# Two transformer blocks on one core: convolution transposes a step later, one step a group in the output norm, Fourier columns first

## The chip, the cores and the metric

The kernel runs on one core of one Trainium2 chip. The metric is the device time in microseconds of one execution; lower is better. Three executions of the kernel before took 2638.27 to 2641.5 us, with a median of 2640.46 us.

## The reference

Two blocks work on a sequence of 256 rows of 2048 float32 values.

The first block is two layers. A layer projects its input to 7680 columns and makes three branches: differential attention (4 heads), dilated attention (8 heads) and a gated convolution of 31 taps with a norm and a pointwise projection. Each branch is gated, the three are joined, projected back, added to the input and normed.

```python
def conformer_conv(u, glu_gate, w_dw, b_dw, ln_g, ln_b, w_pw):
    h = u * jax.nn.sigmoid(glu_gate)
    h = lax.conv_general_dilated(h, w_dw[:, None, :], ...) + b_dw
    h = jax.nn.silu(layer_norm(h, ln_g, ln_b))
    return h @ w_pw
...
    y = jnp.concatenate([ya, yb, yc], axis=-1) @ w_out
    return layer_norm(ALPHA * x + y, ln_g, ln_b)
```

The second block first makes six vectors (shifts, scales, gates) from a condition vector and a large matrix `w_mod`. It norms its input and a context, projects both, and mixes four branches: neighbourhood attention with the context (8 heads), a Fourier transform, pooling windows and a short convolution. Then come a gated merge, a projection and a feed-forward part.

```python
    h = modulate(rms_norm(x, norm1_w[i]), sh1, sc1)
    q, k, v, ft, pool, sv, sb, sc = mixer_inputs(h, w_in[i], q_norm_w[i], k_norm_w[i])
    branches = (neighbourhood_attention(q, k, v, kc, vc, rpb[i]), fourier_mix(ft),
                pool_mix(pool, w_pool[i], pool_scale[i]), short_conv_mix(sv, sb, sc, conv_w[i]))
```

## The kernel before

All large products are "blocks": 256 rows times 512 output columns. A float32 product is made of three fast products: weights and activations are each split in a rounded part `hi` and a rest `lo`, and hi x hi, hi x lo and lo x hi are accumulated in one PSUM bank. So TensorE works through a list of "jobs" (256 rows of a weight block, 12 matmuls of 512 columns), and `run` (L326) issues one step for each: 12 matmuls and what belongs around them.

In a step `run` issues, in this order: `high` (ScalarE rounds the weights of the job four steps ahead, L343), one step of each running task (`step_tasks`, L211), `low` (VectorE makes the rest, L351) and the load of a later weight tile on SP's queue, one product pair of the modulation where the meter leaves room (`wmod_step`, L438), and the step's 12 matmuls, with the block's `pre` ahead of its first and its evacuation behind its last (L374 to L400). Every engine runs its own instructions in the order in which they were issued.

The small work (heads, convolution, norms, transposes) is written as tasks: Python generators whose `yield` ends what they issue in one step. `step_tasks` takes tasks from the front of a queue while the running ones hold under 3 of the PSUM banks kept for them (and enough of the 13 scratch rows), and steps each. `need` (L184) forces a task: all that it has left is issued at once, in the step in which something needs it. All of these groups therefore stand at places in the engines' queues that follow from counts of yields.

The meter: VectorE's and TensorE's estimated times are added up when instructions are issued (L61 to L76), each step lays 1.15 on VectorE's (SPLIT, L359), and `room` (L177) is what is left of a lead of 2.6.

```python
    def room(self):
        return self.t_pe + 2.6 - self.t_dve
```

The modulation: `WMOD_STEPS` (L37) spreads the 32 jobs of each of six chunks over steps. A job of a chunk that begins at a and ends at b is due at a + (b - a) x number/32; it is issued when its step is at or past the due one and the room is at least 1.0 (chunks 0 and 1, two VectorE products a job) or 0.2 (the others, one product), and eight steps past due in any case (L450). Chunk 0 is (22, 146), chunk 1 (160, 274).

Where the change touches:

- `conv` (L925) is the convolution of a layer as a task. The evacuation of the layer's second block adds it (`ev_glu`, L590, which also makes the gated product `sg` on VectorE). It transposes `sg` (L935), copies it to `pad`, then makes 124 tap products, two or four in a step: `if i % 4 == 3 or i % 2 and self.room() < 0.9: yield`, each laid to the meter as 0.33. Then it transposes, norms, transposes back, and makes the pair `cT` (`cTh` at L985 on ScalarE, a yield, `cTl` at L987 on VectorE). The block `conv_pw` (L647) needs that pair: its `pre` forces the task. It is the 13th block of the layer; the 12 ahead of it are 8 steps each. A layer has 154 steps.
- `layer_end` (L690) for layer 1: the task `gen` (L747) norms the layer's output in place (`norm`, L694), multiplies and adds the rows `ln_g` and `ln_b` (`affine`, four VectorE products a group; the rows come by GpSimd's queue, `row`, L711), sums squares (`square`), stores each group (`keep`, L723, also on GpSimd's queue), and then goes on in `rms_t` (L780): sums, scale by ScalarE (`xr`), transposes, and the pairs `hT`. Its steps run beside the four blocks on the context (`kc0`, `vc0`, `kc1`, `vc1`, 32 steps), which are the first of the second block.
- `second` (L991): behind the context blocks come the blocks on `hT`: keys, values, queries of four heads (`k0`, `v0`, `q0`), the Fourier columns (`w[6]`), and keys, values, queries of the other four. The first of them forces `hT` as far as it needs it (`h_pre`). The evacuation of a query block adds four tasks `na_head` (L1045, 23 steps each, after a wait for the normed queries) and a task that forces these heads and then transposes their output. The evacuation of the Fourier block puts two tasks `fourier_groups` (13 steps each) at the front of the queue (L1336).

Of the kernel before, what the change touches and what calls it, by code (L numbers as in the profile page):

```python
# [128 lines left out]
class Kernel:  # L129
# [560 lines left out]
    def layer_end(self, l, r, stats):  # L690
        nc, a = self.nc, self.a
        mv, rs = stats["mv"], stats["rs"]

        def norm(g, t):  # L694
            if len(rs) <= t:
                return None
            if g == 0:
                nc.vector.tensor_scalar(r[g][:, t], r[g][:, t], mv[:, t, 0:1], rs[t][0][:, 0:1],
                                        op0=ALU.subtract, op1=ALU.mult)
            else:  # L700
                nc.scalar.activation(r[g][:, t], r[g][:, t], AF.Identity, scale=rs[t][0][:, 0:1], bias=rs[t][1])
            return r[g][:, t]

        if l == 0 and len(rs) == 1:
            self.xs = self.dp.tile([S, D], F32, name="xs0")
        elif l == 1:
            self.xs = self.dp.tile([S, D], F32, name="xs1")
        xs = self.xs
        rows = {}

        def row(g):  # L711
            if g < 4 and g not in rows:
                rows[g] = []
                for nm_ in ("ln_g", "ln_b"):
                    q = self.h([128, 512], name="row")
                    nc.gpsimd.dma_start(q, a[nm_][l:l + 1, g * 512:(g + 1) * 512].broadcast_to([128, 512]))
                    rows[g].append(q)

        def affine(g, t):
            nc.vector.tensor_tensor(r[g][:, t], r[g][:, t], rows[g][0], op=ALU.mult)  # L720
            nc.vector.tensor_tensor(r[g][:, t], r[g][:, t], rows[g][1], op=ALU.add)

        def keep(g):  # L723
            nc.gpsimd.dma_start(xs[:, g * 512:(g + 1) * 512].rearrange("(t p) f -> p t f", p=128), r[g])

        if l == 0 and len(rs) == 2:
            def gen():
                yield from self.wait(lambda: self.x_task, [self.xT_task])
                for g in range(4):
                    row(g)  # L730
                    yield
                    for t in range(2):
                        while self.room() < 0.6 and not self.x_task.forced:
                            yield
                        affine(g, t)
                        yield
                    keep(g)
            self.x_task = self.add(gen(), banks=0, rows=4)
        elif l == 0:
            self.xT = [self.pair("xT") for _ in range(4)]  # L740
            self.xT_task = self.add(self.split_t(
                [self.t_items(g, self.xT[g], norm, self.col("lng", g * 4, 4), self.col("lnb", g * 4, 4))[t]
                 for g, t in TILES], ahead=2), front=True)
        else:
            ss = self.m([128, 2, 4], name="ss")

            def gen():  # L747
                row(0)
                row(1)
                for g in range(6):  # L750
                    if g < 4:
                        for t in range(2):
                            norm(g, t)
                    if g >= 2:
                        for t in range(2):
                            self.square(r[g - 2][:, t], ss[:, t, g - 2:g - 1])
                        keep(g - 2)
                    yield
                    if 1 <= g < 5:
                        for t in range(2):  # L760
                            affine(g - 1, t)
                        yield
                        rows.pop(g - 1)
                        row(g + 1)
                yield from self.rms_t(r, ss, "sc1", "sh1")
            self.hT = [self.pair("hT") for _ in range(4)]
            self.h_dst = self.hT
            self.hT_task = self.add(gen(), front=True, rows=7)
        self.x_in = xs
# [155 lines left out]
    def conv(self, l, h, st):  # L925
        nc = self.nc
        hp = self.cp.tile([128, 4, 30 + S], F32, name="pad")
        nc.gpsimd.memset(hp[:, :, 0:30], 0.0)
        yield
        for c in range(0, 4, 2):  # L930
            p = self.aux()
            for i in range(2):
                for t in range(2):
                    o = i * 256 + t * 128
                    nc.tensor.transpose(p[:, o:o + 128], h[:, t, (c + i) * 128:(c + i + 1) * 128], self.ident)  # L935
            yield
            nc.scalar.activation(hp[:, c:c + 2, 30:30 + S], p.rearrange("p (c t) -> p c t", c=2), AF.Copy)
            yield
        acc = self.s([128, 4, S], name="cacc")
        st["conv"].banks = 0  # L940
        for i in range(4 * TAPS):
            j, c = divmod(i, 4)
            wj = self.col(f"dw{l}", c * TAPS + j)
            x = hp[:, c, j:j + S]
            if j == 0:
                nc.vector.tensor_scalar(acc[:, c], x, wj, self.col(f"cb{l}", c), op0=ALU.mult, op1=ALU.add)
            else:
                nc.vector.scalar_tensor_tensor(acc[:, c], x, wj, acc[:, c], op0=ALU.mult, op1=ALU.add)
            if i % 4 == 3 or i % 2 and self.room() < 0.9:
                yield  # L950
        yield
        while self.held()[1] >= 3 and not st["conv"].forced:
            yield
        st["conv"].banks = 1
        z = self.s([128, 2, 512], name="z")
        for t in range(2):
            p = self.aux()
            for c in range(4):
                nc.tensor.transpose(p[:, c * 128:(c + 1) * 128], acc[:, c, t * 128:(t + 1) * 128], self.ident)
            yield  # L960
            bn = self.m([128, 6], name="cbn")
            nc.vector.bn_stats(bn, p)
            mv = self.m([128, 2], name="cmv")
            nc.vector.bn_aggr(mv, bn)
            rs = self.rstd(mv[:, 1:2], 1, 1.0, EPS)
            yield
            nm = self.m([128, 1], name="nm")
            nc.vector.scalar_tensor_tensor(nm, mv[:, 0:1], -1.0, rs[:, 0:1], op0=ALU.mult, op1=ALU.mult)
            nc.scalar.activation(z[:, t], p, AF.Identity, scale=rs[:, 0:1], bias=nm)
            yield  # L970
        yield
        cT = self.pair("cT")
        u = self.s([128, 4, S], name="csilu")
        for c in range(0, 4, 2):
            p = self.aux()
            for i in range(2):
                for t in range(2):
                    o = i * 256 + t * 128
                    nc.tensor.transpose(p[:, o:o + 128], z[:, t, (c + i) * 128:(c + i + 1) * 128], self.ident)
            yield  # L980
            for i in range(2):
                nc.scalar.activation(u[:, c + i], p[:, i * 256:(i + 1) * 256], AF.Silu,
                                     scale=self.col(f"cg{l}", c + i), bias=self.col(f"cl{l}", c + i))
            yield
        nc.scalar.activation(cT[0], u, AF.Copy)  # L985
        yield
        nc.vector.tensor_tensor(cT[1], u, cT[0], op=ALU.subtract)  # L987
        st["cT"] = cT


    def second(self):  # L991
        nc, a = self.nc, self.a
        w = a["w_in2"]
# [17 lines left out]
        hsrc = lambda k, t: self.src_of(hT)(k, t)  # L1011
# [64 lines left out]
        def ev_branch(key, fn):  # L1076
            def ev(ps):
                ev_copy(key)(ps)
                bT[key] = self.pair("bT")
                st["t" + key] = fn(st.pop(key), bT[key])  # L1080
            return ev
# [2 lines left out]
                                      (2560, ev_copy("vc1")))):  # L1084
            self.block(w[c0 // 512], csrc, ev, start=start_na if i == 0 else None)
        for g in range(2):
            self.block(w[2 + g], hsrc, ev_norm(f"k{g}"), pre=None if g else h_pre,
                       start=None if g else h_start)
            self.block(w[4 + g], hsrc, ev_copy(f"v{g}"))
            self.block(w[g], hsrc, ev_norm(f"q{g}", heads(g)))  # L1090
            if g == 0:
                self.block(w[6], hsrc, ev_branch("ft", self.fourier))

        def ev_sv(ps):
            x = st["sc"]
# [88 lines left out]
        for n in range(4):  # L1184
            self.block(a["w_o"][n], lambda k, t: self.src_of(yT)(k, t), evac_t=ev_o(n),
                       pre=lambda k: self.need(st[f"m{k // 2}"]), start=load_x(n, r, (3, 4, 5) if n == 3 else ()), tail=TAIL if n == 3 else 0)
# [36 lines left out]
        for part, js in ((0, range(0, 4)), (1, range(4, 8)), (2, range(8, 11))):  # L1223
# [3 lines left out]
            for n in range(4):  # L1227
                self.block(a["w_fd"][n], lambda k, t: self.src_of(aT)(k, t), evac_t=ev_down(part, n),
                           pairs=[2 * j + i for j in js for i in range(2)],
                           pre=lambda k: self.need(st[f"f{k // 2}"]), start=load_x(n, xr),  # L1230
# [302 lines left out]
```

## Time and profile before

| | |
|---|---|
| median of 3 executions | 2640.46 us (2638.27 to 2641.5) |
| profiled execution | 2642.78 us |
| its span | 2640.9 us, mean granted TensorE clock 0.996 |
| TensorE busy | 99% of the span |
| VectorE, ScalarE, GpSimd busy | 68%, 48%, 5% |
| mean DMA | 233 GB/s |

The span goes from the first to the last instruction of the profiled execution; the execution's own time lies around it. PE is TensorE's matmuls, PEld its weight loads, DVE is VectorE, ACT is ScalarE, POOL is GpSimd; a q behind an engine's name is its queue of DMAs. [...] Instructions issued through the meter's helper all carry its line, L75, so they are known by their tiles (out<-in). A number in brackets is the time for which the engine sat idle ahead of the instruction, with what released it. Adjacent equal instructions are merged in a timeline (x4).

### The profile page before, as it was taken

The page shows a single profiled execution, that of the slowest core. Times are in us where ns is not written, and L with a number is a line of the kernel's source. Part 1 is how long each engine was busy: PE and PEld are TensorE (multiplying, and loading weights), DVE is VectorE, ACT ScalarE, POOL GpSimd, SP SyncE. Part 2 cuts the span into 40 slices and gives each one's busy share as a digit, 9 for nine tenths or more (in the row PEclk, how much of TensorE's full clock was granted, in tenths as well). Part 3 has the DMA queues.
Part 4 walks back from the last instruction along what each step waited for, and adds up shares of the span by engine and source line. Part 5 has one row for each costly group of instructions (what it writes and reads, how often), then busy time and mean ns, then how long its engine had stood idle before and what let it go on. Part 6 is the DMA issues. An engine that isn't in the chain of part 4 may idle for free.

```text
span 2640.9 us, 32555 instructions
## 1 busy us (share of the span) xinstructions
PE 2611.5 (99%) x11902; PEld 2155.8 (82%) x11902; DVE 1802.6 (68%) x2516; ACT 1257.7 (48%) x1603; POOL 132.0 (5%) x193
## 2 busy tenths in 40 slices
PE   9999999999999999999999999999999999999999
PEld 7888888778888878887888888888788888888887
DVE  5898777799977788655766677777655554555444
ACT  6444753545466555444454444444544434443442
POOL 0000010000001020100200000000100000001000
PEclk9999999899999999999999999999999999999999
DMA  8776676676666788775776787888655576657664
GB/s 303 244 225 213 212 238 232 194 256 223 216 217 218 266 280 280 249 244 177 240 233 242 236 294 258 291 289 312 222 187 194 187 243 201 193 189 240 226 195 152
DMA packets 171233, 614.69 MB, mean 233 GB/s; under 512 B 19849, under 2 KB 20673, under 8 KB 171073
## 3 DMA queue, kind: packets, MB, share of 16 engines
q1 hardware_dynamic: 158400, 572.59, 64.9%
q0 software_dynamic: 11232, 37.24, 4.4%
q10 hardware_dynamic: 1440, 2.79, 0.3%
q8 instruction: 93, 1.52, 0.2%
q14 instruction: 68, 0.55, 0.1%
HBM read 599.92 MB, written 12.62 MB: 232 GB/s over the span
## 4 chain that ended last, share of the span: by engine, by line
PE 94%; DVE 2%; DMA 2%; issue 1%; POOL 0%; ACT 0%; SPq 0%; DVEq 0%; ACTq 0%; POOLq 0%
PE mm L75 88%; PE aux L75 6%; DMA raw<-in_w_in 1%; DVE lo L351 1%; DMA raw<-in_w_out 1%; DMA row<-in_ln_b 1%; DVE f L75 0%; DVE res L75 0%; ACT hi L343 0%; POOL rstd L229 0%; DVE wmjunk L75 0%; POOL rstd L228 0%; DVE xTl L75 0%; DVE gate L75 0%; DVE h2Tl L75 0%
## 5 line engine op out<-in xcount | busy, mean ns | idle before, releaser
L351 DVE TENSOR_TENSOR lo<-raw,hi 128x1024 fp32r<-128x1024 f32 (+1 forms) x893 | 1077.9, 1220 | 641.8 <-ACT hi L343 640.9
L343 ACT ACTIVATE hi<-raw 128x1024 fp32r<-128x1024 f32 (+1 forms) x893 | 936.6, 1059 | 1028.0 <-PE mm L75 832.1
L75 PE MATMUL mm<-hi,xTh 128*128 128x512 f32 x960 | 385.3, 401 | 6.0 <-ACT hi L343 5.9
L75 PE MATMUL mm<-hi,xTl 128*128 128x512 f32 x960 | 377.2, 393 | 1.1 <-DVE xTl L75 1.1
L75 PE MATMUL mm<-lo,xTh 128*128 128x512 f32 x960 | 376.2, 392 | 0.0
L75 PE MATMUL mm<-hi,hTh 128*128 128x512 f32 x864 | 343.6, 398 | 0.0
L75 PE MATMUL mm<-hi,hTl 128*128 128x512 f32 x864 | 336.9, 390 | 0.0
L75 PE MATMUL mm<-lo,hTh 128*128 128x512 f32 x864 | 336.4, 389 | 0.0
L75 DVE CUSTOM_DVE_ANT_0 wmjunk<-wm,c 128x1024 bf16<-128x1024 f32 x256 | 312.4, 1220 | 4.7 <-DMA wm<-in_w_mod 2.4
L75 PE MATMUL mm<-hi,h2Th 128*128 128x512 f32 x704 | 276.0, 392 | 0.1
L75 PE MATMUL mm<-hi,h2Tl 128*128 128x512 f32 x704 | 274.5, 390 | 1.1 <-DVE h2Tl L75 1.1
L75 PE MATMUL mm<-lo,h2Th 128*128 128x512 f32 x704 | 274.3, 390 | 0.0
L75 PEld LDWEIGHTS mm<-hi,xTh 128*128 128x128 f32 x960 | 181.9, 189 | 43.4 <-ACT hi L343 5.9
L75 PEld LDWEIGHTS mm<-hi,xTl 128*128 128x128 f32 x960 | 181.4, 189 | 41.3 <-DVE xTl L75 2.2
L75 PEld LDWEIGHTS mm<-lo,xTh 128*128 128x128 f32 x960 | 181.9, 189 | 35.9 <-DVE lo L351 0.4
L75 PEld LDWEIGHTS mm<-hi,hTl 128*128 128x128 f32 x864 | 162.2, 188 | 34.4
L75 PEld LDWEIGHTS mm<-lo,hTh 128*128 128x128 f32 x864 | 162.4, 188 | 32.8 <-issue 0.2
L75 PEld LDWEIGHTS mm<-hi,hTh 128*128 128x128 f32 x864 | 162.3, 188 | 32.4 <-issue 0.5
L75 PEld LDWEIGHTS mm<-hi,h2Tl 128*128 128x128 f32 x704 | 132.3, 188 | 29.1 <-DVE h2Tl L75 1.5
L75 PEld LDWEIGHTS mm<-hi,h2Th 128*128 128x128 f32 x704 | 132.4, 188 | 27.5 <-ACT h2Th L284 0.8
L75 PEld LDWEIGHTS mm<-lo,h2Th 128*128 128x128 f32 x704 | 132.4, 188 | 26.9
L75 PE MATMUL mm<-hi,yTh 128*128 128x512 f32 x384 | 150.9, 393 | 0.0
(274 smaller groups left out, 3061.0 us busy)
## 6 DMA issues: line engine op xcount, KB each, us to landing
raw<-in_w_in SPq DMA_DIRECT2D x360, 512.0 KB, 4.4
wm<-in_w_mod SPq DMA_DIRECT2D x192, 512.0 KB, 4.8
raw<-in_w_gate SPq DMA_DIRECT2D x128, 512.0 KB, 4.7
raw<-in_w_fg SPq DMA_DIRECT2D x88, 512.0 KB, 4.4
raw<-in_w_fu SPq DMA_DIRECT2D x88, 512.0 KB, 3.8
raw<-in_w_fd SPq DMA_DIRECT2D x88, 512.0 KB, 4.3
raw<-in_w_out SPq DMA_DIRECT2D x64, 512.0 KB, 4.6
raw<-in_w_o SPq DMA_DIRECT2D x32, 512.0 KB, 5.2
```

What stands on the lines that cost most here:

```text
L75: return f(*args, **kw)
L343: nc.scalar.activation(hi[:, k], t[:, k], AF.Copy)
L351: nc.nc.vector.tensor_tensor(lo[:, k], t[:, k], hi[:, k], op=ALU.subtract)
```

## The change

In `conv` one more `yield` stands ahead of the first transposes. In `layer_end`'s task for layer 1, two of a group's yields become one at the group's end, so that the norm of one group, the squares of another and the products of a third are issued in one step. In `second` the Fourier block moves from behind the first queries to the front of the blocks on `hT`, and takes `pre` and `start` with it.

```diff
@@ -755,13 +755,12 @@
                         for t in range(2):
                             self.square(r[g - 2][:, t], ss[:, t, g - 2:g - 1])
                         keep(g - 2)
-                    yield
                     if 1 <= g < 5:
                         for t in range(2):
                             affine(g - 1, t)
-                        yield
                         rows.pop(g - 1)
                         row(g + 1)
+                    yield
                 yield from self.rms_t(r, ss, "sc1", "sh1")
             self.hT = [self.pair("hT") for _ in range(4)]
             self.h_dst = self.hT
@@ -926,6 +925,7 @@
         nc = self.nc
         hp = self.cp.tile([128, 4, 30 + S], F32, name="pad")
         nc.gpsimd.memset(hp[:, :, 0:30], 0.0)
+        yield
         yield
         for c in range(0, 4, 2):
             p = self.aux()
@@ -1084,12 +1084,11 @@
                                       (2560, ev_copy("vc1")))):
             self.block(w[c0 // 512], csrc, ev, start=start_na if i == 0 else None)
         for g in range(2):
-            self.block(w[2 + g], hsrc, ev_norm(f"k{g}"), pre=None if g else h_pre,
-                       start=None if g else h_start)
+            if g == 0:
+                self.block(w[6], hsrc, ev_branch("ft", self.fourier), pre=h_pre, start=h_start)
+            self.block(w[2 + g], hsrc, ev_norm(f"k{g}"))
             self.block(w[4 + g], hsrc, ev_copy(f"v{g}"))
             self.block(w[g], hsrc, ev_norm(f"q{g}", heads(g)))
-            if g == 0:
-                self.block(w[6], hsrc, ev_branch("ft", self.fourier))
```

## Rows read from the trace of the kernel before

**Rows 1.** page, part 1: busy us, share of the span, instructions
```profile
PE 2611.5 (99%) x11902; PEld 2155.8 (82%) x11902; DVE 1802.6 (68%) x2516; ACT 1257.7 (48%) x1603; POOL 132.0 (5%) x193
```

**Rows 2.** waits of TensorE, whole span: us in total, times, longest us
```profile
PE aux L75 <- ACT xr L792: 7.4, 2, 4.4
...
PE aux L75 <- DVE sg L75: 1.8, 2, 1.6
```

**Rows 3.** chain that ended last, one step: start us, us, what
```profile
910.16 2.76 PE mm L75 x12
```

**Rows 4.** timeline, layer 1's gated product: start us, us, instruction, [idle before <-releaser]
```profile
531.16 0.33 PE L75 MATMUL aux<-ident,sg 128*128 128x128 f32 x1 [1.58 <-DVE sg L75]
...
531.75 0.55 PE L75 MATMUL aux<-ident,sg 128*128 128x128 f32 x3 [0.27 <-DVE sg L75]
```

**Rows 5.** timeline, layer 1, where the convolution ends
```profile
765.59 1.05 ACT L985 ACTIVATE cTh<-csilu 128x1024 fp32r<-128x1024 f32 x1
...
767.12 1.22 DVE L75 TENSOR_TENSOR cTl<-csilu,cTh 128x1024 fp32r<-128x1024 f32 x1
...
770.43 1.28 ACT L623 ACTIVATE gate<-mm 128x512 f32<-128x512 f32 x2 [0.19 <-PE mm L75]
...
771.61 1.05 ACT L343 ACTIVATE hi<-raw 128x1024 fp32r<-128x1024 f32 x1
...
772.42 0.40 PE L75 MATMUL mm<-hi,cTl 128*128 128x512 f32 x1
...
772.69 1.23 DVE L351 TENSOR_TENSOR lo<-raw,hi 128x1024 fp32r<-128x1024 f32 x1 [4.35 <-ACT hi L343]
```

**Rows 6.** timeline of VectorE, layer 1's modulation pairs, 1st and 25th
```profile
509.00 1.22 DVE L75 CUSTOM_DVE_ANT_0 wmjunk<-wm,c 128x1024 bf16<-128x1024 f32 x1
...
759.90 1.22 DVE L75 CUSTOM_DVE_ANT_0 wmjunk<-wm,c 128x1024 bf16<-128x1024 f32 x1
```

**Rows 7.** timeline, layer 0: modulation pairs 1 and 19, and the projection
```profile
71.49 1.22 DVE L75 CUSTOM_DVE_ANT_0 wmjunk<-wm,c 128x1024 bf16<-128x1024 f32 x1
...
285.08 1.22 DVE L75 CUSTOM_DVE_ANT_0 wmjunk<-wm,c 128x1024 bf16<-128x1024 f32 x1
...
296.79 1.05 ACT L343 ACTIVATE hi<-raw 128x1024 fp32r<-128x1024 f32 x1
...
297.61 0.40 PE L75 MATMUL mm<-hi,cTl 128*128 128x512 f32 x1
```

**Rows 8.** windows: start:end length, busy PE, PEld, DVE, ACT, POOL, clock, DMA, GB/s
```profile
983.00:986.40 3.40, 0.42 (x3) 0.15 (x2) 2.04 (x2) 0.93 (x2) 3.10 (x4) 1.00 0.58 186
...
1899.00:1906.00 7.00, 5.25 (x20) 3.97 (x20) 6.44 (x16) 5.71 (x10) 1.92 (x4) 0.51 0.74 249
```

**Rows 9.** timeline of TensorE, two waits of transposes for scaled rows
```profile
986.25 0.66 PE L75 MATMUL aux<-ident,xr 128*128 128x128 f32 x4 [2.98 <-ACT xr L792]
...
1900.51 2.82 PE L75 MATMUL aux<-ident,xr 128*128 128x128 f32 x12 [4.40 <-ACT xr L792]
```

**Rows 10.** timeline, first context block and the output norm
```profile
947.75 0.39 PE L75 MATMUL mm<-hi,hcTh 128*128 128x512 f32 x1
...
957.34 2.02 DVE L75 TENSOR_TENSOR res<-res,row 128x512 f32<-128x512 f32 x3 [1.09 <-DMA row<-in_ln_b]
...
962.69 2.74 DVE L75 TENSOR_TENSOR res<-res,row 128x512 f32<-128x512 f32 x4
...
979.76 0.21 DVE L75 TENSOR_REDUCE tot<-ss 128x1 f32<-128x4 f32 x2
```

**Rows 11.** timeline, the second block's first heads
```profile
1203.14 0.48 DVE L75 TENSOR_SCALAR qk<-aux,qns 128x256 f32<-128x256 f32 x1 [3.40 <-PE aux L75]
...
1203.66 0.47 ACT L1276 ACTIVATE qk<-aux,cols 128x256 f32<-128x256 f32 x1 [0.36 <-DVE qk L75]
...
1244.79 0.66 PE L75 MATMUL aux<-ident,sc 128*128 128x128 f32 x4 [1.64 <-ACT sc L1295]
...
1246.14 0.71 PE L75 MATMUL aux<-v,pt 128*128 128x128 f32 x4 [0.69 <-ACT pt L1303]
```

## Prediction

> **What bounds the kernel now.** I read the page first: TensorE is busy 2611.5 of 2640.9 us, so 29.4 us idle [rows 1]. Then the list of what TensorE waited for: besides the start and the layer ends, the places that the edits touch are the scaled rows of the norm (7.4 us in two waits, of which one is touched) and the gated convolution input (1.8 us) [rows 2]. So the time is matrix work plus waits in TensorE's own queue. No edit adds or drops an instruction on any engine; each only places groups of them elsewhere in queues that run in program order. What must be asked of each is which group now stands behind something late. I count the scheduler's steps in the code (one step is 12 large matmuls, 2.76 us [rows 3]) and fix them to the trace where a group shows; step 0 is the first of a layer, or of the second block's own projections.
>
> **Edit 1, convolution one step later.** What it gives: in layer 1 the transposes stand at step 17 and wait 1.58 and 0.27 us for the gated product [rows 4]; those are both of the waits of this kind [rows 2], so layer 0 gives nothing. A step later the product is there. Gain 1.85 us; the bound the other way is 0.
>
> What it costs lies at the other end. The taps take two a step: the meter leaves a room of at most 2.6 - 1.15 - 2 x 0.33 = 0.79, under 0.9, so 124 taps are 62 steps, 21 to 82, and nothing in the loop can catch up. From there the steps are fixed: cTh is issued in step 95 and cTl in step 96. The block that reads the pair, the pointwise projection, begins in step 96 (12 blocks of 8 lie before it). The trace agrees: cTl is the last thing before step 96's weight split, at 767.12, while the first matmul that reads it starts at 772.42; it has 4.1 us to spare [rows 5]. One step later, cTh is issued in step 96 and cTl is forced by the block itself, behind all that step 96 has queued. On ScalarE that is the gate's evacuation, which cannot start before TensorE ends step 95 (770.43, 1.28 us), then the weight split of 771.61 (1.05 us) [rows 5]: cTh runs at about 772.7 to 773.7. On VectorE it is the split of 772.69 and then a pair of modulation products: the pair at 759.90 is the 25th since 509.00 [rows 6], so the next, number 25 counted from 0, falls due at 160 + 114 x 25/32 = 249.06, and step 96 of layer 1 is slot 250. Before, cTl itself took the room that step 96 had; now it is not yet counted and 1.45 is free, over the 1.0 asked. So VectorE goes 773.8 + 2 x 1.22 = 776.3, and cTl ends at 777.5: 5.1 us after TensorE wants it. All of this is on TensorE's path: the three products accumulate in one bank in that order, and everything behind them on its queue waits. Layer 0 is the same: pair 285.08 is the 19th since 71.49, the next is due at 22 + 124 x 19/32 = 95.6, and the split of 296.79 and the matmul at 297.61 [rows 7] lie as in layer 1. Bounds: without the pair in front 2.6 us each; above, half a step more, 6.5, as the convolution's last activations move into step 95, ahead of the gate on ScalarE.
>
> **The clock.** Idle of this length has a second price. [...] The new wait is 5.1 us with two matmuls in it, nearest to the 4.40, so I add half of 5.25, 2.6 us, each; the bound below is 0. [...]
>
> So edit 1: -1.85 + 2 x (5.1 + 2.6) = +13.6 us.
>
> **Edit 2, the norm in one step a group.** Six steps instead of ten before the row sums. It removes the 2.98 us wait of the transposes at 986.25, which came from sums taken at 979.76 and then queued on GpSimd behind another task [rows 9, 10]: the sums now come before that task. But VectorE gets four affine products (2.74 us) and a weight split (1.23) in each of four steps in a row, 3.9 us against TensorE's 2.76. The start does not move: the bias row lands at 957.34 as before (GpSimd issues it at the same place), and three products follow to 959.4 [rows 10]. The splits of steps 1 to 4 of the first context block then end at about 960.5, 964.4, 968.2 and 972.1. TensorE uses them four steps on, from 947.75 + 2.76 k [rows 10]: at 961.8, 964.5, 967.3 and 970.1 for k = 5 to 8 (second matmul of each). So it waits 0.9 and, after that, 1.1 us: 2.0. The weight loads start late with the splits, and the first scaled rows stand on ScalarE behind a split of such a load: 0.5 to 1.8 us more at step 9, taken as 1.2. GpSimd's own queue (row loads, stores of the output) keeps its order; each store waits for the same products as before. Sum 3.2 - 2.98 = +0.2; bounds -2.98 (all of it covered by the four steps in hand) and +5 (the last row, loaded behind the first store, lands late and the clock falls too).
>
> **Edit 3, Fourier first.** The two Fourier tasks ran between the second block's heads 0 to 2 and the pass that transposes their output. They move to steps 10 to 19 of the block, with three steps between the issue of their table loads and the first use; cost 0, or one wait of a step at most if a table came late. But they were what held two of the three task slots while head 3 ran. In the kernel before, the pass starts at step 63, when head 3 has done half, and forces the other half: TensorE waits 1.64 and 0.69 us [rows 11]. Now heads 0 and 1 end at step 57, and at step 58 head 3 and the pass start together, so the pass forces the whole head: the same two waits for its first half, 2.33, and before them the copies of its q and k, 0.48 on VectorE and then 0.47 on ScalarE with hand-overs [rows 11], 1.1. Its bias loads are on GpSimd's queue, which has nothing else there and issues them when their buffers come free, not when TensorE gets to the step: 0. +3.4 us; bounds 0 and +6. The second group has the same order of tasks behind the pool block in both kernels: 0. SP's queue keeps one weight load a step; only whose it is changes.
>
> **Sum.** 13.6 + 0.2 + 3.4 = +17.2 us. The profiled execution took 2642.78 us (span 2640.9), 2.3 over the median 2640.46 of the three runs; it goes to 2660.0, the median to 2657.6. A difference under 0.2% (5.3 us) can't be told from none.
>
> **Rivals.**
> - Clock stays up through both new waits: 2652.4. For it the 2.98 us row and the two matmuls inside the wait; against it the 4.40 us row. Chance 0.19.
> - The modulation pair is not in front of cTl (it depends on the meter's room to a tenth): 2.6 for 5.1 twice, 2652.6. Chance 0.10.
> - The norm is dearer: VectorE is the bound for longer, about 5 us: 2662.4. For it the load that lands at 957.34 with VectorE waiting; against it that modulation products are held back meanwhile. Chance 0.12.
> - Not slower: the pair is in time. Its place is step 96, its price 15.4 us, and it decides at cTl's end before 772.42. It needs ScalarE to run cTh ahead of the gate's evacuation, or a tap step that takes four taps. Then -1.85 + 0.2 + 3.4 = +1.8, 2642.2: no change. Only the 4.1 us to spare speaks for it, more than one step. Chance 0.12.
> - Beyond that, all the waits named go and none comes: -1.85 - 2.98 - 2.33 = -7.2, 2633.3. That the Fourier tasks leave would have to let head 3 end first, and their slots are filled at once. Chance 0.06.
>
> **How the numbers follow.** The forecast has 0.41. Faster is the last rival, 0.06; within 0.2% the one before, 0.12; the rest, 0.82, is slower. The range runs from 2644, where clock and pair are both cheap, to 2666, the dear norm with its bound on the head; it leaves out the last two rivals, 0.18.
>
> **What would show it.** Right: waits of the pointwise matmuls on cTh and then cTl in both layers, about 5 us each, clock rows under 1 behind them; no wait on the gated product; none of 2.98 us before the norm's transposes but small ones on weight splits before; two pairs of 1.64 and 0.69 where one was at the first heads. Wrong: pointwise matmuls that start with no wait, which takes 15 us of the 17 away.

## The result and the profile after the change

The changed kernel takes 2674.52 us (median of three executions, 2674.44 to 2674.63) where the kernel before takes 2640.85 on the same chip, so 33.7 us more by the medians. The ratio is 1.0124 with a 95% interval of 1.011 to 1.0138, which is 32.7 us, 29.0 to 36.4. A fourth execution ran at a granted clock of 0.749 of full speed, took 3307.47 us and is left out. Forecast were 17.2 us more, with a range up to 2666. The direction was right, the size about half, and the time lies outside the range.

The changed kernel's page, part 1 (busy us, share of the span, instructions), to be set beside [rows 1]:

```profile
PE 2621.8 (98%) x11902; PEld 2161.1 (81%) x11902; DVE 1802.9 (67%) x2516; ACT 1258.8 (47%) x1605; POOL 129.7 (5%) x193
```

TensorE issues the same 11902 instructions and is busy 10.3 us longer with them: that is work at a lower clock (mean granted clock 0.990, before 0.996). ScalarE has two instructions more (1605 for 1603), both loads of activation tables of 1.28 us, so the prediction's "No edit adds or drops an instruction on any engine" is off by two; the repaired kernels below have two more still (1607) and are faster, so these loads are not the cost. The rest of the 31.8 us by which the span grew (2640.9 to 2672.7) is idle time. The waits of TensorE in the changed kernel, whole span (us in total, times, longest us), answer to [rows 2]:

```profile
PE aux L75 <- ACT qk L1275: 6.9, 1, 6.9
...
PE mm L75 <- DVE cTl L75: 5.8, 2, 3.1
PE aux L75 <- ACT sc L1294: 5.7, 3, 2.4
PE aux L75 <- ACT xr L791: 5.4, 2, 4.4
PE mm L75 <- ACT cTh L985: 4.6, 2, 2.3
```

The wait on the gated product `sg` is gone, and `xr` is down from 7.4 to 5.4: the gains that were named. `cTh` and `cTl`, 10.4 us in two layers, are the pair that was forecast to be late. The longest new wait, 6.9 us for `qk`, stands where the prediction had 1.1.

**Where it goes, stage by stage.** Set the same evacuations of the two traces side by side: layer 0's pointwise projection puts the changed kernel 7.8 us behind, the gated product of layer 1 gives 2.0 back, layer 1's projection costs 7.3; the start and the turn of the layer give 1.7 back in small pieces, at which nothing was changed. Over the norm and the context blocks the lag is 11.4 us at the start and 11.3 at the end. From there to the gates of the second block it grows by 20.1 us, to 31.4, where it stays. The terms of the prediction for these stages were 7.7, -1.85, 7.7, +0.2 and +3.4: four hold within half a microsecond, and the last is off by 16.7.

**Layer 0's projection.** The changed kernel's timeline where the convolution ends (start us, us, instruction, [idle before <-releaser]), against [rows 5, 7]:

```profile
296.09 1.08 ACT L623 ACTIVATE gate<-mm 128x512 f32<-128x512 f32 x2
...
298.00 1.06 ACT L985 ACTIVATE cTh<-csilu 128x1024 fp32r<-128x1024 f32 x1
298.15 1.23 DVE L351 TENSOR_TENSOR lo<-raw,hi 128x1024 fp32r<-128x1024 f32 x1 [6.05 <-ACT hi L343]
299.12 0.50 PE L75 MATMUL mm<-hi,cTh 128*128 128x512 f32 x1 [2.31 <-ACT cTh L985]
...
300.55 1.23 DVE L75 CUSTOM_DVE_ANT_0 wmjunk<-wm,c 128x1024 bf16<-128x1024 f32 x1
...
301.70 1.22 DVE L75 TENSOR_TENSOR cTl<-csilu,cTh 128x1024 fp32r<-128x1024 f32 x1
...
302.98 0.79 PE L75 MATMUL mm<-hi,cTl 128*128 128x512 f32 x1 [3.13 <-DVE cTl L75]
```

The order is the forecast one: `cTh` behind the gate's evacuation and a weight split on ScalarE, `cTl` behind a weight split and the modulation pair on VectorE. The two waits are 5.44 us together; 5.1 was predicted. The matmul at 302.98 takes 0.79 us instead of 0.40 [rows 7], and the windows of the changed kernel (length, busy PE, PEld, DVE, ACT, POOL, granted clock as a share of full speed, DMA share, GB/s) say why:

```profile
299.00:301.00 2.00, 0.73 (x2) 0.30 (x2) 1.97 (x4) 1.97 (x5) 0.00 (x0) 0.82 0.31 74
301.00:303.00 2.00, 0.02 (x1) 0.02 (x1) 2.00 (x4) 1.31 (x3) 0.00 (x0) 0.50 0.66 219
```

**The heads.** The changed kernel's timeline where head 3 of the first group runs, against [rows 11]:

```profile
1150.04 0.60 ACT L1019 ACTIVATE q<-mm 128x512 f32<-128x512 f32 x1 [3.70 <-PE mm L75]
...
1230.03 0.60 ACT L1019 ACTIVATE q<-mm 128x512 f32<-128x512 f32 x1 [5.45 <-PE mm L75]
...
1236.86 0.38 PE L75 MATMUL aux<-ident,kc 128*128 128x128 f32 x2
...
1237.07 0.38 PE L75 MATMUL aux<-ident,q 128*128 128x128 f32 x2
...
1237.27 0.60 ACT L1020 ACTIVATE sq<-mm 128x512 f32<-128x512 f32 x1 [6.65 <-PE aux L75]
...
1239.82 1.23 DVE L351 TENSOR_TENSOR lo<-raw,hi 128x1024 fp32r<-128x1024 f32 x1 [11.50 <-ACT hi L343]
...
1243.50 0.48 DVE L75 TENSOR_SCALAR qk<-aux,qns 128x256 f32<-128x256 f32 x1
...
1244.02 0.47 ACT L1275 ACTIVATE qk<-aux,cols 128x256 f32<-128x256 f32 x1 [1.98 <-DVE qk L75]
1244.54 1.22 PE L75 MATMUL aux<-qk 128*128 128x256 f32 x2 [6.87 <-ACT qk L1275]
...
1248.26 1.11 PE L75 MATMUL aux<-ident,sc 128*128 128x128 f32 x4 [1.64 <-ACT sc L1294]
1250.06 1.22 PE L75 MATMUL aux<-v,pt 128*128 128x128 f32 x4 [0.69 <-ACT pt L1302]
...
1255.48 1.12 PE L75 MATMUL aux<-ident,sc 128*128 128x128 f32 x4 [1.64 <-ACT sc L1294]
1257.29 1.22 PE L75 MATMUL aux<-v,pt 128*128 128x128 f32 x4 [0.69 <-ACT pt L1302]
```

Read it from 1230.03 (the first line, the first group's queries, is used further below). The second group's query block has just ended, and its evacuation (`ev_norm`, key `q1`) squares the result into a tile `sq` (L1020). ScalarE copies the first half at 1230.03, and then stands 6.65 us: what releases it is TensorE, which transposes tiles of the first group for head 3 from 1236.86 on. No data goes from there to `sq`. That is the mark of a buffer: by the code `sq` gets one of the 24 slots of the `s` pool, and a tile of the first group still holds it. It is the context keys `kc`: their two transposes end at 1237.24 and the square starts at 1237.27, while those of `q` and `k` still run. Behind `sq` on ScalarE stand the rest of the evacuation, three weight roundings, `kk` and half of `qk`; VectorE waits 11.50 us for one of those roundings, and its half of `qk` (1243.50) stands behind two weight splits and a modulation product there. So `qk`, which head 3 needs next and whose task is forced whole in this step, is 6.87 us late. After it come the two pairs 1.64 and 0.69 that were forecast. In this trace ScalarE keeps the order of issue: no rounding passes the waiting square in the 6.65 us, and the three follow from 1238.72 on without a gap.

The clock of the changed kernel behind that, and TensorE's wait and clock at the second group's pass (timeline; windows, columns as above):

```profile
1411.61 0.66 PE L75 MATMUL aux<-ident,sc 128*128 128x128 f32 x4 [2.43 <-ACT sc L1294]
```

```profile
1244.00:1262.00 18.00, 12.80 (x39) 9.63 (x40) 5.33 (x13) 4.24 (x8) 0.00 (x0) 0.50 0.16 58
...
1413.00:1416.40 3.40, 3.40 (x12) 3.11 (x13) 1.36 (x2) 0.85 (x1) 0.00 (x0) 0.50 0.01 5
```

Before, the clock was 1.00 throughout these stretches (1150 to 1250 and 1380 to 1430 us in that trace). The 20.1 us can now be summed from rows: waits in the head 11.5 less the 2.33 of before, 9.2; 12.80 us of work at half clock, half of it lost, 6.4, and 0.4 at the edge; at the second pass a wait of 2.43 and one of 0.69 where 0.69 was, 2.4, and half of 3.40 us of work at half clock, 1.7. Together 20.1.

### The profile page after: what moved, and what is told of

It is laid out like the page before. It is cut to its first block, busy times and chain, and to the rows that moved or that the text cites. A ratio compares the mean times of both kernels' runs of the same rounds, so it can differ in the third digit from the quotient of the medians.

```text
span 2672.7 us, 32558 instructions
## 1 busy us (share of the span) xinstructions
PE 2621.8 (98%) x11902; PEld 2161.1 (81%) x11902; DVE 1802.9 (67%) x2516; ACT 1258.8 (47%) x1605; POOL 129.7 (5%) x193
## 4 chain that ended last, share of the span: by engine, by line
PE 94%; DVE 2%; ACT 1%; DMA 1%; issue 1%; POOL 0%; SPq 0%; ACTq 0%; DVEq 0%; POOLq 0%
PE mm L75 89%; PE aux L75 6%; DMA raw<-in_w_in 1%; DVE lo L351 1%; ACT hi L343 1%; DVE f L75 0%; DMA raw<-in_w_out 0%; DMA row<-in_ln_b 0%; DVE wmjunk L75 0%; DVE res L75 0%; ACT L850 0%; ACT L982 0%; DVE xTl L75 0%; ACT L623 0%; DVE cTl L75 0%
```

## The experiments

All times are against the kernel before on the same chip (median 2641.08 for the edits one at a time and the late squares; 2641.36 for the four-step squares and the last three runs; 2642.03 for the others); a difference in us is the ratio less 1 times that median. Where a text on record numbers an edit, 1 is the convolution, 2 the norm, 3 the Fourier columns.

**One edit at a time.** Edit 1 alone:

```diff
         nc.gpsimd.memset(hp[:, :, 0:30], 0.0)
         yield
+        yield
```

> The kernel before with edit 1 alone (one more step at the start of the convolution). Theory (the pair is late by about 5 us in each layer and the clock falls after it, as the trace after the change shows: 7.8 us in layer 0, 7.3 in layer 1, 2.0 gained at the gated product): +13 us, 2653 to 2655. Rival (the three edits only cost this together, because the norm and the Fourier block shift the same buffers): under +6.

Measured: ratio 1.006 (1.0046 to 1.0074), +15.8 us, 12.1 to 19.5; the profiled execution's span is 13.8 over that of before. The waits of TensorE in this run:

```profile
PE mm L75 <- DVE cTl L75: 5.3, 2, 2.6
PE mm L75 <- ACT cTh L986: 4.6, 2, 2.3
```

The same two waits as in the changed kernel, and no wait on `sg`. The +13 of the theory lies inside the interval, if below its middle; the part stands by itself.

Edit 2 alone:

```diff
                         keep(g - 2)
-                    yield
                     if 1 <= g < 5:
...
                             affine(g - 1, t)
-                        yield
                         rows.pop(g - 1)
                         row(g + 1)
+                    yield
```

> The kernel before with edit 2 alone (the norm in one step a group). Theory (the sums come before the other task on GpSimd, so the 2.98 us wait of the transposes goes, and about as much comes back on the weight splits and the scaled rows): -1 to +1 us. Rival (the waits that come back were caused by the later convolution in the same task list, so alone the edit keeps its gain): -3 us.

Measured: ratio 1.0003 (0.9994 to 1.0012), +0.8 us, -1.6 to +3.2. The wait of 2.98 us [rows 9] is gone, and the timeline of TensorE in this run shows what came for it:

```profile
966.68 0.50 PE L75 MATMUL mm<-lo,hcTh 128*128 128x512 f32 x1 [0.73 <-DVE lo L351]
...
970.48 0.50 PE L75 MATMUL mm<-lo,hcTh 128*128 128x512 f32 x1 [0.78 <-DVE lo L351]
...
974.33 0.66 PE L75 MATMUL aux<-ident,xr 128*128 128x128 f32 x4 [1.06 <-ACT xr L791]
```

2.6 us in three pieces: a wait split up, not removed. The rival (-3) falls.

Edit 3 alone:

```diff
         for g in range(2):
+            if g == 0:
+                self.block(w[6], hsrc, ev_branch("ft", self.fourier), pre=h_pre, start=h_start)
...
-            if g == 0:
-                self.block(w[6], hsrc, ev_branch("ft", self.fourier))
```

> The kernel before with edit 3 alone (Fourier columns first). Theory (q1's squares on ScalarE wait 6.65 us for the buffer that head 3's transposes free, the forced head waits 11.5 us in sum where it waited 2.33, and the clock is at half for some 20 us after): +18 to +21 us, with a wait near 6.9 for the copy of qk. Rival (the prediction's own price, a forced head with ScalarE free): +3.4 us and no wait over 2 us there.

Measured: ratio 1.0072 (1.0057 to 1.0086), +19.0 us, 15.1 to 22.7, with the wait of 6.87 us for `qk` again. The prediction's own price, +3.4, falls. The three parts give 15.8 + 0.8 + 19.0 = 35.6 against 32.7 for the whole by its ratio: they add, within their intervals.

**What in edit 3 costs it.** The buffer can be taken out of the way without touching the forcing: q1's squares are taken from its copy in SBUF, and later, when head 3 already stands ahead of them in every queue.

```diff
-                    nc.scalar.activation(sq[:, t], ps[t], AF.Square)
+                    if key != "q1":
+                        nc.scalar.activation(sq[:, t], ps[t], AF.Square)
...
                     yield
+                    if key == "q1":
+                        yield
+                        for t in range(2):
+                            nc.scalar.activation(sq[:, t], x[:, t], AF.Square)
+                        yield
```

> Edit 3 alone, with q1's squares taken from its copy one step after head 3 has been issued, so that ScalarE never stands for the buffer; the head is still forced whole in one step. Theory (the buffer is the larger part): the 6.65 us wait on ScalarE goes, the wait for qk falls to about 2 us, and of the +20 some +5 to +12 are left, according to whether the clock still falls. Rival (the forced chain and its clock are the cost, the buffer only a place where the wait shows): +17 to +20 as in edit 3 alone.

Measured: ratio 1.0029 (1.002 to 1.0039), +7.7 us, 5.3 to 10.3. TensorE's timeline in the head and at the second group's pass, and the two stretches of the head at half clock (windows):

```profile
1228.74 0.70 PE L75 MATMUL aux<-qk 128*128 128x256 f32 x2 [1.08 <-ACT qk L1281]
...
1231.51 0.66 PE L75 MATMUL aux<-ident,sc 128*128 128x128 f32 x4 [1.64 <-ACT sc L1300]
...
1396.83 0.66 PE L75 MATMUL aux<-ident,sc 128*128 128x128 f32 x4 [0.98 <-ACT sc L1300]
```

```profile
1233.00:1236.40 3.40, 3.40 (x12) 2.66 (x12) 0.68 (x2) 0.00 (x0) 0.00 (x0) 0.50 0.00 0
1239.80:1243.20 3.40, 3.40 (x13) 3.01 (x13) 1.78 (x4) 0.61 (x1) 0.00 (x0) 0.50 0.00 0
```

This is the head that the prediction described: 1.08 for `qk` (1.1 was predicted), then 1.64, 0.69, 1.64, 0.69, in sum 5.74, less the 2.33 of before 3.4, to the tenth what was predicted. What was left out is the clock, half of 6.80 us of work, 3.4, and 1.0 us more of waits at the second pass: 7.8 in sum, for 7.7 measured.

The other 11 us of edit 3 go with the square's wait. By the trace of edit 3 alone, in which 9.5 us of work in the head and 6.1 at the second pass lie at half clock, they are 5.8 for `qk`, 1.3 of clock behind it, and at the second pass, which comes two steps later in the run with the late squares, 1.4 of waits and 3.1 of clock: 11.6. No run gave the pool one more slot: that the wait is for a slot rests on the releaser in the trace and on this run.

Then the forcing was taken away too, on top of the edits above: the pass gives head 3 up to fourteen steps before it forces, and the squares come twelve steps late.

```diff
+                    for _ in range(14):
+                        if all(t.done for t in ta) or st[f"ta{g}"].forced:
+                            break
+                        yield
                     for t in ta:
                         self.need(t)
```

> Edit 3 alone, but the pass that forces head 3 waits up to fourteen steps before it forces, and q1's squares are taken twelve steps after its copy: head 3 runs over the steps in which it ran before, half of it forced as before, and ScalarE never stands for the buffer. The Fourier columns stay first. Theory (all that edit 3 costs is head 3: forced, then held by the buffer, then at half clock): within 2 us of the kernel before. Rival (taking the Fourier columns first costs something of its own, in the loads or in the first two steps of the block): +5 to +8, as the run with the squares late alone.

Measured: ratio 1.0011 (1.0002 to 1.002), +2.9 us, 0.5 to 5.3: neither number cleanly. The stretch of head 3 has no wait, but the timeline shows a new one, at the pool branch:

```profile
1403.55 1.22 PE L75 MATMUL aux<-z,wpool 128*128 128x256 f32 x2 [3.16 <-ACT z L1384]
```

The reading was that the squares, twelve steps late, had pushed the second group of heads back, and with it the pool's tasks into the step that forces them. With four steps instead of twelve (`range(4)` for the squares, the rest as above) the heads clear that step:

> The run with head 3 spread, with q1's squares four steps late instead of twelve. In that run a wait of 3.16 us and one of 0.53 stood at the pool branch's z near 1403 us, where the delayed second group of heads had pushed the pool's tasks into the step that forces them, and the clock was at half over 1402 to 1412; no wait stood in the whole stretch of head 3. Theory (its +3 us is this wait, made by the delay, and the Fourier columns first cost nothing of their own): no wait at z, -2 to +1 us against the kernel before. Rival (the Fourier order costs +3 somewhere that the waits do not show): +3 again.

Measured: ratio 0.9988 (0.998 to 0.9997), -3.2 us, -5.3 to -0.8, with no wait for `z`. Over the 60 us in which the changed kernel loses most, TensorE has not a moment idle in this run (windows):

```profile
1200.00:1260.00 60.00, 60.00 (x293) 50.24 (x292) 38.20 (x52) 28.34 (x34) 2.75 (x2) 1.00 0.70 233
```

A head 3 that is not forced also saves the 2.33 us that it waited in the kernel before, which is most of the -3.2. So the order of the blocks costs nothing of its own. All of edit 3's price is head 3 and the second pass: forced, held by a buffer, at half clock.

**What in edit 1 costs it.** First the modulation pair, put off by a step where the low part of `cT` is late:

```diff
+            if self.slot in (96, 250):
+                return
             if self.slot < due or (self.room() < (1.0 if chunk < 2 else 0.2) and self.slot < due + 8):
                 return
```

> Edit 1 alone, with the pair of modulation products (1.22 us each on VectorE) put off by one step at the two steps in which the low part of cT is late. Theory (the pair is what stands between the two waits; the clock falls by the first wait of 2.3 us already, as the trace of edit 1 alone shows 0.67 over 298 to 300 us): the wait for cTl falls from 2.65 us to some 0.4, the one for cTh and the half clock stay, about 2.4 us less in each layer: +8 to +11 against the kernel before. Rival (the clock only falls because of the two waits together): +2 to +5.

Measured: ratio 1.0033 (1.0021 to 1.0045), +8.7 us, 5.5 to 11.9, against +15.8 with the pair. TensorE's timeline, layer 0, and a window of the same run:

```profile
299.60 0.69 PE L75 MATMUL mm<-hi,cTh 128*128 128x512 f32 x1 [2.31 <-ACT cTh L988]
...
301.05 0.79 PE L75 MATMUL mm<-hi,cTl 128*128 128x512 f32 x1 [0.33 <-DVE cTl L75]
```

```profile
300.00:302.00 2.00, 1.67 (x4) 0.83 (x3) 1.11 (x2) 1.99 (x6) 0.00 (x0) 0.50 0.56 145
```

The second wait goes, the first stays, and the clock falls after 2.31 us of idle time alone. The theory holds: the pair is worth about 3.5 us a layer (2.4 was expected, and the two intervals allow it), the wait for `cTh` and the clock behind it the rest.

Then the lateness itself: three steps at the end of the convolution are made one.

```diff
                 nc.scalar.activation(u[:, c + i], p[:, i * 256:(i + 1) * 256], AF.Silu, ...
-            yield
+            if c == 0:
+                yield
         nc.scalar.activation(cT[0], u, AF.Copy)
-        yield
         nc.vector.tensor_tensor(cT[1], u, cT[0], op=ALU.subtract)
```

> Edit 1 with two of the steps at the end of the convolution taken out (the last silu, cT's high part and its low part in one step), so that the transposes still come a step later but cT is whole before the step that needs it. Theory (edit 1's whole cost is cT late in step 96, and its gain at the gated product stands): no waits for cT, -1 to -3 us against the kernel before. Rival (the taps a step later delay VectorE's other work as well): +3 or more with no wait for cT.

Measured: ratio 0.9993 (0.9984 to 1.0002), -1.8 us, -4.2 to +0.5. No wait for `cT` is left, nor one for `sg`. The size is the predicted gain of the gated product, though the interval also takes in no change.

**Putting it together.** All three edits, with the convolution's end in one step and the squares behind head 3 (the edits of the run with the late squares and of the run just told):

> All three edits, with the convolution's end in one step and q1's squares a step behind head 3. Theory (the parts add: about -2 for the convolution, 0 to +1 for the norm, +7.7 for the head forced whole): +5 to +8 us against the kernel before, 2646 to 2650. Rival (some of the 33.7 us comes from the edits together and not from these two waits): over +12.

Measured: ratio 1.0022 (1.0012 to 1.0031), +5.8 us. Of the 32.7 us some 27 are gone with these two repairs. And with head 3 spread as well (four steps for the squares):

> All three edits, with the convolution's end in one step, q1's squares four steps late and head 3 spread over the steps. Theory (the three waits are all that the change costs): -3 to +1 us against the kernel before. Rival (parts of the change cost something together): +4 or more.

Measured: ratio 0.9975 (0.9966 to 0.9984), -6.6 us, -9.0 to -4.2: faster than both kernels, and by more than expected: the expectation had not counted that a spread head also saves the 2.33 us that it waited before, as in the run with four steps. TensorE's waits in this run:

```profile
PE mm L75 <- DVE lo L351: 2.2, 3, 0.7
...
PE aux L75 <- ACT pt L1313: 0.7, 1, 0.7
```

`cT`, `sg`, `qk` and `sc` are gone. What is left of the change's own is the norm's split-up wait (`lo`); the 0.7 for `pt` at the second pass was there before.

Last, whether the Fourier columns and the norm are needed for that. The kernel before with edit 1, its end in one step, and a pass that doesn't force its heads:

```diff
-                    for t in ta:
-                        self.need(t)
+                    yield from self.wait(lambda: st[f"ta{g}"], ta)
```

> The kernel before with edit 1, the convolution's end in one step, and a pass over the heads that does not force them; norm and Fourier columns as before. Theory (the waits at the gated product, 1.8, at the heads, 2.33, and at the second pass, 0.7, go, and none comes): -4 to -6 us. Rival (unforced heads finish late and something else is forced): 0 or more, with a new wait behind the heads.

Measured: ratio 0.9979 (0.997 to 0.9988), -5.5 us, as expected. With edit 2 as well:

> The same with edit 2 as well (the norm in one step a group). Theory (edit 2 moves its wait and is worth nothing): as without it, -3 to -6 us. Rival (with the convolution in time the norm's gain of 3 us comes through): -7 to -9.

Measured: ratio 0.9977 (0.9968 to 0.9986), -6.1 us; edit 2 is worth nothing here either. The three last versions can't be told apart; all are about a quarter of a per cent faster than the kernel before. Two waits of TensorE on small tasks are gone in all of them, 1.85 us at the gated product and 2.33 at the first heads; in the last two the 0.69 of the second pass is gone as well.

## Why the prediction was right where it was, and where it failed

- **Edit 1, right in place and size.** The pair is late in step 96 of both layers, by the mechanism and in the order given: 5.44 us of waits in layer 0 for 5.1, and 7.8 and 7.3 us with the clock for 7.7. The gated product gave 2.0 for 1.85. The clock's price, taken from the 4.40 us row and against the 2.98 us row, came out: 7.8 less 5.44 is 2.4 for 2.6. The 2.6 is the prediction's own estimate, half of the 5.25 us of work in the window of the 4.40 us wait, which has the clock at 0.51 [rows 8, 9]; no run shows that term for one wait of 5.1 us, and what the runs showed in its place are these 2.4 us, with the clock at 0.50 over 301 to 303 us, behind waits of 2.31 and 3.13. The reason for the choice, that 5.1 us is nearer to 4.40 than to 2.98, is not what the runs show: without the pair the clock fell behind 2.31 us (0.50 over 300 to 302), less than the 2.98 that had left it at 1.00, so that the number came out is in part luck. The rivals "clock stays up", "no pair in front of `cTl`" and "the pair is in time" fell with it.
- **Edit 2, right.** Predicted were 2.0 us on the splits and 1.2 on `xr` for the 2.98 removed; measured 1.5, 1.06, and no change in the time. The rival "the norm is dearer" fell.
- **Edit 3, the step that failed.** "at step 58 head 3 and the pass start together, so the pass forces the whole head: ... +3.4 us; bounds 0 and +6." It measured +19.0 alone and 20.1 in the whole. That head 3 would be forced whole was right, the two pairs of 1.64 and 0.69 stand in the trace, and the chain was sized to the tenth, as the run with the late squares shows: 5.74 less 2.33. Three things were not in the sum. The largest is the buffer: of the 19.0 us, 11 go when the square no longer waits for it (clock and second pass included). The step looked at the queues that head 3 passes and not at what its lateness keeps in use. Then the clock: half clock was priced for the convolution's waits, but not for the head, where a string of waits from 0.69 to 1.64 us was enough (3.4 us without the buffer's wait; with it 4.7 in the run of edit 3 alone and 6.8 in the changed kernel). And the second group, set to 0 because its tasks keep their order: in the changed kernel 2.4 us of waits and 1.7 for the clock, less when the pass came two steps later. An upper bound of 6 was not a bound, because it only took the forced chain into account.
- **It could have been seen.** In the kernel before, the queries' evacuations of the two groups and head 3's transposes of `kc` are these lines of the timeline:

```profile
1106.58 0.60 ACT L1019 ACTIVATE q<-mm 128x512 f32<-128x512 f32 x1 [3.70 <-PE mm L75]
...
1196.08 0.38 PE L75 MATMUL aux<-ident,kc 128*128 128x128 f32 x2
...
1216.01 0.60 ACT L1019 ACTIVATE q<-mm 128x512 f32<-128x512 f32 x1 [6.29 <-PE mm L75]
1216.51 0.59 ACT L1020 ACTIVATE sq<-mm 128x512 f32<-128x512 f32 x1
```

  The square does not wait, and `kc` has been read 20.0 us earlier, at 1196.46. (A square that does not wait doesn't show whose slot it takes; the reckoning takes it to be the one of `kc`, as in the changed kernel.) The change takes the eight jobs of the Fourier block out from between q0's block and q1's, 8 x 2.76 = 22 us [rows 3], already more than the 20. By the traces it is 29.4 with the small work that went along (109.4 us between the two evacuations before, 80.0 after), and head 3 starts 2.7 us earlier, counted from q0's evacuation (89.5 before, 86.8 after): 20.0 + 2.7 - 29.4 = -6.7, the wait of 6.65. So q1's evacuation comes ahead of head 3's transposes. The prediction counted those steps for the pass, and not for q1.

## What to carry to other kernels

When a block moves, count again, for every tile allocated after it, which earlier reader has to be done before its slot is free: here an evacuation that came ahead of a late reader stopped ScalarE for 6.65 us, and TensorE behind it for 6.87. A forced chain and the buffers that it holds are one price and not two, and the half clock behind a string of short waits belongs in it (3.4 us behind waits of 0.69 to 1.64 us in the run with the late squares). And a task may be a step later for nothing if its last steps, which only hand work from one engine to the next, can be issued together, as in the run with the convolution's end in one step (-1.8 us, -4.2 to +0.5).

## What the runs showed of the clock that was not expected

Nearly the same wait at the same place sent the clock down in one execution and not in another, and kept it there for 7 us in one and for 13 in another. At the turn of layer 0 the kernel before, the changed kernel and the runs with the late squares and with the convolution's end in one step have a wait of 2.73 to 2.75 us for `res`. In the run with the late squares, which issues TensorE's instructions in the same order as the kernel before up to this point and past the norm, the timeline and the windows show

```profile
472.47 1.94 PE L75 MATMUL aux<-ident,res 128*128 128x128 f32 x8 [2.73 <-DVE res L75]
```

```profile
472.00:478.00 6.00, 4.88 (x19) 3.86 (x19) 6.00 (x16) 4.11 (x7) 0.98 (x2) 0.50 0.70 226
478.00:480.00 2.00, 1.28 (x4) 0.30 (x2) 2.00 (x6) 1.46 (x3) 0.00 (x0) 0.85 0.00 0
```

and in the kernel before, after a wait of 2.74 us at 472.85, the windows show

```profile
472.00:486.00 14.00, 11.85 (x35) 8.58 (x36) 13.92 (x35) 9.26 (x13) 1.36 (x3) 0.51 0.38 124
486.00:488.00 2.00, 2.00 (x10) 1.58 (x9) 1.97 (x7) 0.00 (x0) 0.00 (x0) 1.00 0.82 254
```

so some 7 us at half clock in the one and 13 in the other. The norm's wait of 2.98 us left the clock at 1.00 in the kernel before [rows 8]; in the run with the late squares it is 3.24 us, and the clock is at 0.50 behind it:

```profile
986.00:988.00 2.00, 2.00 (x6) 1.57 (x6) 1.46 (x2) 2.00 (x4) 0.00 (x0) 0.50 0.17 66
```

A wait of 1.58 us on `sg` [rows 4] left the clock at 1.00 before; in the run of edit 3 alone, again with the same instructions up to there, one of 1.49 did not (windows, the kernel before and that run):

```profile
532.00:534.00 2.00, 2.00 (x12) 1.66 (x11) 0.83 (x1) 1.31 (x2) 0.00 (x0) 1.00 0.90 274
532.00:534.00 2.00, 2.00 (x7) 1.51 (x6) 0.00 (x0) 0.20 (x1) 0.00 (x0) 0.50 0.74 277
```

So the rise to full clock, near 479 us in the one and at 486 in the other, differs between these executions, and so does the fall. Of these waits of 1.5 to 3.2 us the clock's price is known as an expectation only, and single runs of one kernel here spread over up to 11 us (2636.66 to 2647.81 for the kernel before). A difference of 5 us needs several runs, and a wait that one profile shows as cheap can be dear in the next, as the one for `sg` was.
